# The low halves of 598 weight tiles: a negated copy on ScalarE and an accumulating DMA in place of a subtraction on VectorE

## The chip, the cores and the metric

The kernel runs on one core of a Trainium2 chip. The time is the device time of one execution in microseconds (us), lower is better. A core has a matmul engine (PE, with its weight loads shown apart as PEld), three engines for elementwise work (DVE is VectorE, ACT is ScalarE, POOL is GpSimd) and SP, which here only issues DMAs. POOL issues DMAs too; these go through the queue that the profile calls q0, software_dynamic, while SP's go through q1, hardware_dynamic. All queues share 16 DMA engines.

## The reference, cut to what matters

Two layers of a diffusion backbone on 512 latent and 256 context tokens with 1024 features, all float32. Each layer is a half-step SwiGLU FFN, a token mixer (a gated MLP in the first layer, attention in the second), and a second half-step FFN; every sublayer is modulated and closed by a layer norm.

```python
def swiglu(h, w_in, w_out):
    g, u = jnp.split(h @ w_in, 2, axis=-1)
    return (jax.nn.silu(g) * u) @ w_out

def ffn_sublayer(x, shift, scale, gate, w_in, w_out, ln_g, ln_b):
    y = swiglu(modulate(x, shift, scale), w_in, w_out)
    return layer_norm(ALPHA * x + 0.5 * gate * y, ln_g, ln_b)
...
        x_lat = ffn_sublayer(x_lat, ..., ffn_w_in[i, 0], ffn_w_out[i, 0], ...)
        x_ctx = ffn_sublayer(x_ctx, ..., ffn_w_in[i, 0], ffn_w_out[i, 0], ...)
        y_lat = gqa_mix(...) if is_attn else gmlp_mix(...)
        x_lat = layer_norm(ALPHA * x_lat + m_lat[5] * y_lat, ...)
        x_lat = ffn_sublayer(x_lat, ..., ffn_w_in[i, 1], ffn_w_out[i, 1], ...)
```

The output is the latent stream after both layers, so the last FFN runs on 512 tokens alone.

## The kernel before

A float32 operand is split in a high part, rounded to the type fp32r in which PE multiplies fast, and a low part, the rest. A product is three matmuls: high by high, high by low, low by high. Weights are split on the way. A unit is a 128x512 piece of a weight matrix, 256 KB: SP loads it into one of six `raw` buffers (`load_raw`), ScalarE copies it into the first half of one of eight `w` buffers (`split_later`, the copy of line 155), and VectorE subtracts that from `raw` into the second half (line 156). The subtraction is put in a list and written out at the next `flush`. The buffer `w` is free again when PE has multiplied with it, `raw` when both passes have read it. `units` yields the units in the order in which PE wants them, from a list of jobs that `__init__` makes: ("u", sources) is a plain run of pieces; "s" and "r" are Strassen steps of the FFN's first matrix, in which seven products take the place of eight and some units are sums made by VectorE (`sums`). Sources of `ffn_w_in` and of the first half of `gmlp_w_in` are cut as four runs of 128 floats for each of 128 partitions (runs of 512 bytes); sources of the output matrices, of `attn_w_qkv` and of gMLP's second half have rows of 2 KB.

PE's, SP's and POOL's instructions stay in the order in which the program writes them; a scheduler orders those of VectorE and ScalarE. POOL issues the DMAs of activations that are spilled and read back (`act<-stage`, `q<-act`), all-reduces and adds the pieces of the modulation vectors (`acc`, `mod`), raises variances to a power for the layer norms (`rs`), and issues the accumulating DMAs of the last residual (`zsum`, a buffer in DRAM, line 484).

The order of the work: a start of 100 us (modulation and the first units), layer 0's first FFN in Strassen steps to 370 us and its output matrix to 555, the gated MLP to 1157, layer 0's second FFN to 1730, layer 1's first to 2210, attention to 2440, and the last FFN, which has no Strassen steps ("latent FFN"), to 2817.

Of the kernel before, what the change touches and what calls it, by code (L numbers as in the profile page):

```python
# [8 lines left out]
F32R = mybir.dt.float32r  # L9
AF = mybir.ActivationFunctionType  # L10
ALU = mybir.AluOpType
AX = mybir.AxisListType

P = 128
D = 1024
KD = D // P
# [8 lines left out]
D_FF = 2816  # L25
# [14 lines left out]
W_BUFS = 8  # L40
# [53 lines left out]
class Backbone:  # L94
# [93 lines left out]
    def weight_order(self):  # L188

        io = self.io
        jobs = []

        def ffn(l, s, strassen=True, kernel_start=False):
            wi = io["ffn_w_in"][l, s].rearrange("(k p) f -> p k f", p=P)
            wo = io["ffn_w_out"][l, s]

            def cut(o, f, half):
                return wi[:, 4 * half : 4 * half + 4, o + f * P : o + f * P + P]  # L200

            start = FIRST_OPEN + SECOND_OPEN if kernel_start else OPEN
            if strassen:
                jobs.append(("u", [cut(0, f, half) for f, half in start]))
            for f in range(FF):
                if strassen:
                    srcs = [cut(0, f, 0), cut(D_FF, f, 0), cut(D_FF, f, 1), cut(0, f, 1)]
                    jobs.append(("r" if f < OPENED else "s", srcs))
                else:
                    jobs.append(("u", [cut(o, f, half) for o in (0, D_FF) for half in range(2)]))  # L210
            if strassen:
                through(wo, FF)
            else:
                order = Acts.orders(FF, KEPT_LAT, READ_BACK_LAT)[0]
                out(wo, order[:-CLOSE_LAT], 1)
                out(wo, order[-CLOSE_LAT:], CLOSE_LAT)

        def piece(wo, f, half):
            return wo[f * P : f * P + P, half * 512 : half * 512 + 512]

        def out(wo, order, n):
            for x in range(0, len(order), n):
                jobs.append(("u", [piece(wo, f, half) for half in range(2) for f in order[x : x + n]]))

        def through(wo, n):
            for half, order in enumerate(Acts.orders(n, KEPT, READ_BACK)):
                jobs.append(("u", [piece(wo, f, half) for f in order]))

        wm = io["w_mod"][0].rearrange("(k p) f -> p k f", p=P)
        quarter = lambda q: [  # L230
            wm[:, 2 * j : 2 * j + 2, i * D + q * 256 : i * D + q * 256 + 256] for i in (1, 0) for j in range(4)
        ]
        ffn(0, 0, True, True)
        first = jobs.pop(0)[1]
        start = quarter(0) + quarter(1) + quarter(2) + first[0:2] + quarter(3) + first[2:]
        jobs.insert(0, ("u", start))
        wi = io["gmlp_w_in"][0]
        for cc in range(GMLP_HALF // 512):
            o = GMLP_HALF + cc * 512
            jobs.append(("u", [wi[k * P : k * P + P, o : o + 512] for k in range(KD)]))  # L240
        wi = wi.rearrange("(k p) f -> p k f", p=P)
        us = lambda j: [wi[:, 4 * half : 4 * half + 4, j * P : j * P + P] for half in range(2)]
        for j in range(GMLP_CH):
            jobs.append(("u", us(j)))
        through(io["gmlp_w_out"][0], GMLP_CH)
        ffn(0, 1)
        ffn(1, 0)
        wq = io["attn_w_qkv"][0]
        for o in (1024, 0, 512):
            jobs.append(("u", [wq[k * P : k * P + P, o : o + 512] for k in range(KD)]))  # L250
        for h in (0, 4):
            out(io["attn_w_o"][0], range(h, h + 4), 4)
        ffn(1, 1, False)
        self.wsrc = [s for _, srcs in jobs for s in srcs]
        self.wraw, self.wready, self.wlive, self.raw_live, self.reserve = [], [], 0, 0, 0
        self.unit = self.units(jobs)

    def load_raw(self):
        while self.raw_live < RAW_BUFS and self.wsrc:
            src = self.wsrc.pop(0)  # L260
            raw = self.main.tile([P, 512], F32, tag="raw", bufs=RAW_BUFS, name="raw")
            dst = raw if len(src.shape) == 2 else raw[:, :].rearrange("p (a b) -> p a b", b=src.shape[2])
            self.sp.dma_start(dst, src)
            self.wraw.append(raw)
            self.raw_live += 1

    def take(self):
# [7 lines left out]
    def sums(self):  # L275
        return self.main.tile([P, 512], F32, tag="sums", bufs=2, name="sums")

    def unit_of(self, src):
        w = self.main.tile([P, 2, 512], F32R, tag="w", bufs=W_BUFS, name="w")
        self.split_later(w[:, 0], w[:, 1], src, w)  # L280
        if not self.slots:
            self.flush()
        return w

    def units(self, jobs):
        dve, w = self.dve, None
        for kind, srcs in jobs:
            if kind == "u":
                for _ in srcs:
                    w = self.unit_of(self.take())  # L290
                    self.drop(1)
                    yield w
                continue
            g1 = self.take()
            if kind == "s":
                yield self.unit_of(g1)
            u1, u2 = self.take(), self.take()
            if any(key is w for key, _ in self.lows):
                self.flush()
            s1, s2 = self.sums(), self.sums()  # L300
            dve.tensor_tensor(s1, u1, u2, ALU.add)
            dve.tensor_tensor(s2, s1, g1, ALU.subtract)  # L302
            yield self.unit_of(s2)
            dve.tensor_tensor(u1, g1, u1, ALU.subtract)
            w = self.unit_of(u1)
            self.drop(2)
            yield w
            yield self.unit_of(s1)
            g2 = self.take()
            if kind == "s":  # L310
                yield self.unit_of(g2)
            w = self.unit_of(u2)
            self.drop(1)
            yield w
            dve.tensor_tensor(s2, g2, s2, ALU.subtract)
            w = self.unit_of(s2)
            self.drop(1)
            yield w
# [207 lines left out]
    def need(self, *units):  # L526
        for u in units:
            while u not in self.mod_done:
                self.fill()
# [853 lines left out]
    def attention(self, l, i, nblocks, end, prev):  # L1383
# [172 lines left out]
        def step():  # L1556
            if queue and next(queue[0], self) is self:
                queue.pop(0)
                step()

        for n in range(len(units)):
            if n < 12 and n % 3 == 1:
                q_norm(1, n // 3)
            if n + AHEAD < len(units):
                sc = scores(n + AHEAD)
                todo = probs(n, state.pop(n))
                for f in todo:
                    f()
                state[n + AHEAD] = softmax(*sc)
            else:  # L1570
                for f in probs(n, state.pop(n)):
                    f()
# [486 lines left out]
```

## Time and profile before

| | us |
|---|---|
| median of 3 runs | 2817.7 (2817.39 to 2819.66) |
| span of the profiled execution | 2816.9 |
| PE busy | 2771.2 |
| VectorE busy | 2101.1 |
| ScalarE busy | 1163.0 |
| POOL busy | 537.4 |

The profiled execution has no other time beside its span, which lies 0.8 us below the median of the runs. A group's row names line, engine, operation and tiles (written, then read), the count, the busy time, the mean of one in ns, and the idle time of the engine ahead of it with what ended it. In a row of windows stand the stretch, its length, the busy time of each engine with its instructions, the granted PE clock, the DMA share and GB/s. A row of waits says who waited for whom: microseconds in all, times, longest. A row of the timeline starts with the start time and the length of a run of like instructions.

### The profile page before, as it was taken

The numbers are of one execution on the slowest core, as the hardware profiler recorded it, in microseconds if no ns is written. First come the engines' busy times: TensorE is split into PE (matmuls) and PEld (weight loads), VectorE is DVE, ScalarE is ACT, GpSimd is POOL, SyncE is SP. The second block draws the span as 40 slices with busy tenths as digits, with TensorE's granted clock in tenths as the row PEclk, the third lists the DMA queues.
The fourth block names the chain that finished last, engine by engine and source line by source line (L and its number), as shares of the span: only waits on it lengthen the run. The fifth ranks groups of instructions, "written<-read, shape, count | busy, mean of one in ns | idle before, by whom it ended". The sixth has DMA issues, their size and how long they took to land.

```text
span 2816.9 us, 40812 instructions
## 1 busy us (share of the span) xinstructions
PE 2771.2 (98%) x14478; PEld 2501.4 (89%) x14478; DVE 2101.1 (75%) x3681; ACT 1163.0 (41%) x2245; POOL 537.4 (19%) x605
## 2 busy tenths in 40 slices
PE   7999999999999999999999999999999999999998
PEld 5999988888899988899999889999988888888886
DVE  6988879587687776698888759888886598733445
ACT  6433432442355532463334236333432666623321
POOL 1001044333321232200102220000242121000001
PEclk9999999999999999999999999999999999999999
DMA  7443366366565474344336534434595524454352
GB/s 232 131 135 122 112 225 211 114 199 198 184 180 167 150 237 140 123 148 139 121 121 200 181 113 133 144 120 124 154 314 152 148 69 88 132 150 132 113 168 82
DMA packets 398819, 429.99 MB, mean 153 GB/s; under 512 B 28504, under 2 KB 288024, under 8 KB 398616
## 3 DMA queue, kind: packets, MB, share of 16 engines
q1 hardware_dynamic: 364504, 319.40, 37.0%
q0 software_dynamic: 34112, 108.00, 12.4%
q8 instruction: 113, 1.85, 0.3%
q14 instruction: 90, 0.74, 0.1%
HBM read 366.10 MB, written 63.41 MB: 152 GB/s over the span
## 4 chain that ended last, share of the span: by engine, by line
PE 86%; DVE 5%; issue 3%; ACT 3%; DMA 1%; POOL 1%; SPq 0%; DVEq 0%; POOLq 0%; ACTq 0%
PE ps L89 86%; DVE w L89 1%; DMA raw<-in_w_mod_dram 1%; PE pp L89 1%; POOL acc L383 0%; POOL rs L184 0%; ACT z L1957 0%; DMA raw<-in_ffn_w_in_dram 0%; DVE comb L89 0%; DVE w L156 0%; ACT h L601 0%; ACT p L1473 0%; ACT w L155 0%; ACT w L89 0%; DVE nm L1465 0%
## 5 line engine op out<-in xcount | busy, mean ns | idle before, releaser
L89 PE MATMUL ps<-comb,w 128*128 128x384 f32 x5544 | 972.2, 335 | 9.8 <-DVE q L89 2.6
L89 PEld LDWEIGHTS ps<-comb,w 128*128 128x128 f32 x5544 | 961.1, 188 | 16.8 <-DVE w L89 3.8
L89 PE MATMUL ps<-w,acts 128*128 128x512 f32 (+1 forms) x3792 | 860.1, 388 | 0.0
L89 PEld LDWEIGHTS ps<-w,acts 128*128 128x128 f32 x3792 | 707.3, 188 | 145.0
L89 ACT CAST w<-raw 128x512 fp32r<-128x512 f32 x630 | 387.7, 620 | 819.9 <-PE ps L89 723.2
L89 DVE TENSOR_TENSOR w<-raw,w 128x512 fp32r<-128x512 f32 x630 | 454.8, 729 | 260.0 <-ACT w L89 259.9
L89 PE MATMUL ps<-h,w 128*128 128x384 f32 (+2 forms) x2304 | 445.1, 353 | 0.2 <-DVE w L156 0.2
L89 PEld LDWEIGHTS ps<-h,w 128*128 128x128 f32 x2304 | 402.4, 188 | 37.8 <-DVE w L156 0.4
L89 DVE SCALAR_TENSOR_TENSOR acc<-mraw,cs,acc 128x512 f32<-128x512 f32 x378 | 279.2, 772 | 20.3 <-DMA mraw<-in_w_mod_dram 19.8
L89 PE MATMUL ps<-w,h 128*128 128x512 f32 x1200 | 274.6, 390 | 0.0
L383 POOL PARTITION_ALL_REDUCE acc<-acc x56 | 204.8, 3660 | 351.4 <-DVE acc L89 331.3
L89 PEld LDWEIGHTS ps<-w,h 128*128 128x128 f32 x1200 | 224.6, 188 | 46.3
L89 POOL DMA_DIRECT2D act<-stage x84 | 48.4, 576 | 973.5 <-DVE stage L89 934.6
L89 DVE TENSOR_TENSOR q<-q,ps 128x384 f32<-128x384 f32 (+1 forms) x258 | 143.7, 557 | 106.5 <-PE ps L89 89.3
L89 ACT CAST w<-sums 128x512 fp32r<-128x512 f32 x198 | 122.8, 620 | 237.8 <-DVE sums L302 118.1
L89 POOL DMA_DIRECT2D q<-act x226 | 129.0, 625 | 466.1 <-DVE acts L89 308.4
L89 ACT CAST acts<-q 128x384 fp32r<-128x384 f32 (+1 forms) x262 | 127.3, 519 | 78.9 <-DVE q L89 44.2
L89 DVE TENSOR_TENSOR acts<-q,acts 128x384 fp32r<-128x384 f32 (+1 forms) x262 | 145.5, 588 | 8.3 <-ACT acts L89 8.3
L89 DVE TENSOR_TENSOR w<-sums,w 128x512 fp32r<-128x512 f32 x198 | 140.2, 708 | 1.9 <-ACT w L89 1.9
L156 DVE TENSOR_TENSOR w<-raw,w 128x512 fp32r<-128x512 f32 x114 | 75.8, 688 | 28.8 <-ACT w L155 28.4
L184 POOL TENSOR_TENSOR rs<-ve,mhalf 128x1 f32<-128x1 f32 (+3 forms) x47 | 39.1, 831 | 274.8 <-DVE ve L181 167.7
L155 ACT CAST w<-raw 128x512 fp32r<-128x512 f32 x114 | 68.1, 627 | 48.3 <-PE ps L89 25.5
(203 smaller groups left out, 2162.4 us busy)
## 6 DMA issues: line engine op xcount, KB each, us to landing
raw<-in_ffn_w_in_dram SPq DMA_DIRECT2D x400, 256.0 KB, 3.0
mraw<-in_w_mod_dram SPq DMA_DIRECT2D x256, 256.0 KB, 3.5
raw<-in_ffn_w_out_dram SPq DMA_DIRECT2D x176, 256.0 KB, 3.4
q<-act POOLq DMA_DIRECT2D x216, 192.0 KB, 4.3
act<-stage POOLq DMA_DIRECT2D x74, 384.0 KB, 2.9
raw<-in_gmlp_w_in_dram SPq DMA_DIRECT2D x96, 256.0 KB, 3.3
zhat<-z POOLq DMA_DIRECT2D x26, 512.0 KB, 2.9
raw<-in_gmlp_w_out_dram SPq DMA_DIRECT2D x48, 256.0 KB, 2.9
```

Source lines behind the costliest of these rows:

```text
L89: return self.tc.keep_in_program_order(f(*args, **kwargs))
L155: self.act.copy(hi, src)
L156: self.lows.append((key, lambda: self.dve.tensor_tensor(lo, src, hi.bitcast(F32), ALU.subtract)))
L184: self.last_rstd = self.nc.gpsimd.tensor_tensor(rs, ve, self.mhalf[:, 0:1].to_broadcast([P, n]), ALU.pow).ins
L383: nc.gpsimd.partition_all_reduce(accs[c], accs[c], P, bass_isa.ReduceOp.add)
```

## The change

For 598 of the units the second half is made in another way. ScalarE writes the negated high half into it (a second pass, with a scale of −1, rounded as the first), and then POOL issues a DMA that reads the raw piece from DRAM once more and adds it there: raw − high. The units are all pieces of the plain jobs (kind "d" now) and the three unsummed ones of a Strassen step, g1, g2 and u2; the start's units, the Strassen sums and u1 stay with VectorE. 312 of the new DMAs have rows of 2 KB, 286 have four runs of 512 bytes for a partition.

```diff
-                    jobs.append(("u", [cut(o, f, half) for o in (0, D_FF) for half in range(2)]))
+                    jobs.append(("d", [cut(o, f, half) for o in (0, D_FF) for half in range(2)]))
...
         def out(wo, order, n):
             for x in range(0, len(order), n):
-                jobs.append(("u", [piece(wo, f, half) for half in range(2) for f in order[x : x + n]]))
+                jobs.append(("d", [piece(wo, f, half) for half in range(2) for f in order[x : x + n]]))
...
-            self.wraw.append(raw)
+            self.wraw.append((raw, src))
...
+    def unit_from(self, raw, src):
+        w = self.main.tile([P, 2, 512], F32R, tag="w", bufs=W_BUFS, name="w")
+        self.act.copy(w[:, 0], raw)
+        self.act.mul(w[:, 1], raw, -1.0)
+        low = w[:, 1] if len(src.shape) == 2 else w[:, 1].rearrange("p (a b) -> p a b", b=src.shape[2])
+        self.pool.dma_start(low, src, accum_op=ALU.add)
+        return w
...
-            if kind == "u":
+            if kind in ("u", "d"):
                 for _ in srcs:
-                    w = self.unit_of(self.take())
+                    raw, src = self.take()
+                    w = self.unit_of(raw) if kind == "u" else self.unit_from(raw, src)
...
-                yield self.unit_of(g1)
+                yield self.unit_from(g1, src)
...
-                yield self.unit_of(g2)
-            w = self.unit_of(u2)
+                yield self.unit_from(g2, src)
+            w = self.unit_from(u2, second)
```

POOL's order where layer 1 passes from the first FFN to attention, before: `rs` are the powers of the layer norm, `zsum` the last residual, which begins here with its bias.

```order
L184 TENSOR_TENSOR rs_21189<-ve_21188,mhalf 128x1
L184 TENSOR_TENSOR rs_21274<-ve_21273,mhalf 128x1
L89 DMA zsum_21297<-in_ln_b_dram 128x1024
L89 DMA zsum_21298<-in_ln_b_dram 128x1024
L89 DMA zsum_21299<-in_ln_b_dram 128x1024
L89 DMA zsum_21300<-in_ln_b_dram 128x1024
L484 DMA zsum_21297<-zraw 128x512
```

The same place in the changed kernel, where `w` is the second half of a unit:

```order
L184 TENSOR_TENSOR rs_21617<-ve_21616,mhalf 128x1
L89 DMA w<-in_attn_w_qkv_dram 128x512 x2
L184 TENSOR_TENSOR rs_21708<-ve_21707,mhalf 128x1
L89 DMA zsum_21731<-in_ln_b_dram 128x1024
L89 DMA w<-in_attn_w_qkv_dram 128x512 x4
L89 DMA zsum_21732<-in_ln_b_dram 128x1024
L89 DMA zsum_21733<-in_ln_b_dram 128x1024
L89 DMA zsum_21734<-in_ln_b_dram 128x1024
L495 DMA zsum_21731<-zraw 128x512
```

Six of the attention's first low halves now stand in POOL's order around the last power of the layer norm and the first bias.

ScalarE's order where attention ends and the latent FFN opens, before: line 155 is the copy of a unit, 1957 and 1947 normalise a token block (`z`), 601 modulates and 615 makes the tile `h` that PE multiplies.

```order
L1957 ACTIVATE z<-z,nb,rs_23701 128x1024
L615 CAST h<-q 128x4x128
L155 CAST w<-raw 128x512 x6
L601 ACTIVATE q<-ps,modB,modA 128x128 x8
L615 CAST h<-q 128x4x128 x2
L155 CAST w<-raw 128x512
L1947 ACTIVATE z<-z,nb,rs_23789 128x1024
L155 CAST w<-raw 128x512
```

And in the changed kernel (282 and 283 are the two passes of a unit, 1968 and 1958 the normalisations, 612 and 626 the modulation and `h`):

```order
L1968 ACTIVATE z<-z,nb,rs_24167 128x1024
L626 CAST h<-q 128x4x128
L282 CAST w<-raw 128x512
L283 ACTIVATE w<-raw 128x512
L282 CAST w<-raw 128x512
L283 ACTIVATE w<-raw 128x512
L282 CAST w<-raw 128x512
L283 ACTIVATE w<-raw 128x512
L282 CAST w<-raw 128x512
L283 ACTIVATE w<-raw 128x512
L612 ACTIVATE q<-ps,modB,modA 128x128
L1958 ACTIVATE z<-z,nb,rs_24259 128x1024
```

Where six copies stood ahead of the next token block's modulation there are four units of two passes, and the next normalisation now stands ahead of the rest of them.

More of the change, by code (lines that the diff above doesn't have):

```diff
@@ L222, in out @@
             for x in range(0, len(order), n):
-                jobs.append(("u", [piece(wo, f, half) for half in range(2) for f in order[x : x + n]]))
+                jobs.append(("d", [piece(wo, f, half) for half in range(2) for f in order[x : x + n]]))
         def through(wo, n):
             for half, order in enumerate(Acts.orders(n, KEPT, READ_BACK)):
-                jobs.append(("u", [piece(wo, f, half) for f in order]))
+                jobs.append(("d", [piece(wo, f, half) for f in order]))
         wm = io["w_mod"][0].rearrange("(k p) f -> p k f", p=P)
@@ L239, in weight_order @@
             o = GMLP_HALF + cc * 512
-            jobs.append(("u", [wi[k * P : k * P + P, o : o + 512] for k in range(KD)]))
+            jobs.append(("d", [wi[k * P : k * P + P, o : o + 512] for k in range(KD)]))
         wi = wi.rearrange("(k p) f -> p k f", p=P)
@@ L243, in weight_order @@
         for j in range(GMLP_CH):
-            jobs.append(("u", us(j)))
+            jobs.append(("d", us(j)))
         through(io["gmlp_w_out"][0], GMLP_CH)
@@ L249, in weight_order @@
         for o in (1024, 0, 512):
-            jobs.append(("u", [wq[k * P : k * P + P, o : o + 512] for k in range(KD)]))
+            jobs.append(("d", [wq[k * P : k * P + P, o : o + 512] for k in range(KD)]))
         for h in (0, 4):
@@ L293, in units @@
                 continue
-            g1 = self.take()
+            g1, src = self.take()
             if kind == "s":
-                yield self.unit_of(g1)
-            u1, u2 = self.take(), self.take()
+                yield self.unit_from(g1, src)
+            (u1, _), (u2, second) = self.take(), self.take()
             if any(key is w for key, _ in self.lows):
@@ L308, in units @@
             yield self.unit_of(s1)
-            g2 = self.take()
+            g2, src = self.take()
             if kind == "s":
-                yield self.unit_of(g2)
-            w = self.unit_of(u2)
+                yield self.unit_from(g2, src)
+            w = self.unit_from(u2, second)
             self.drop(1)
```

## The prediction

> **What bounds the kernel now.** I read the busy shares first, then the same numbers by stretch, then the chain of waits, the groups, the DMA issues, and last the timeline at the places where the matmul engine changes its work.
>
> ```profile
> span 2816.9 us, 40812 instructions
> PE 2771.2 (98%) x14478; PEld 2501.4 (89%) x14478; DVE 2101.1 (75%) x3681; ACT 1163.0 (41%) x2245; POOL 537.4 (19%) x605
> ...
> 100.00:2790.00 2690.00, 2676.94 (x13938) 2424.63 (x13938) 2010.78 (x3512) 1093.74 (x2108) 519.89 (x576) 1.00 0.49 152
> ...
> 2460.00:2560.00 100.00, 100.00 (x466) 83.80 (x465) 38.45 (x59) 29.24 (x49) 10.37 (x13) 1.00 0.52 153
> 2560.00:2690.00 130.00, 130.00 (x576) 107.63 (x575) 52.77 (x79) 42.80 (x71) 7.41 (x8) 1.00 0.39 118
> ...
> ACT w L89 <- PE ps L89: 803.2, 342, 14.3
> ...
> PEld ps L89 <- DVE w L156: 10.1, 22, 0.8
> ```
>
> PE is the bound: between 100 and 2790 us it is idle 2690 − 2676.9 = 13.1 us, at a granted clock of 1.00. So VectorE, though 75% busy, holds PE up almost nowhere: PE's weight load waits for low halves (the VectorE subtraction at line 156) 10.1 us in all, while ScalarE's copies wait 803.2 us for PE to free a weight buffer. Taking 598 subtractions off VectorE can therefore win at most those 13.1 us and a few at the start. What can be lost is larger: a low half that lands late stops PE, which has nothing else to do.
>
> **The change, part by part.** Of the weight units, 630 of them in the largest group below and the rest like them on other lines, 598 get their second half in the new way.
>
> ```profile
> L89 ACT CAST w<-raw 128x512 fp32r<-128x512 f32 x630 | 387.7, 620 | 819.9 <-PE ps L89 723.2
> L89 DVE TENSOR_TENSOR w<-raw,w 128x512 fp32r<-128x512 f32 x630 | 454.8, 729 | 260.0 <-ACT w L89 259.9
> ...
> L383 POOL PARTITION_ALL_REDUCE acc<-acc x56 | 204.8, 3660 | 351.4 <-DVE acc L89 331.3
> ...
> L484 POOL DMA_DIRECT2D zsum<-zraw x8 | 7.0, 872 | 66.2 <-DVE nm L1467 33.8 <-DVE zraw L477 14.4 <-DMA zsum<-q 7.2
> ...
> zsum<-in_ln_b_dram POOLq DMA_DIRECT2D x4, 512.0 KB, 10.3
> zsum<-zraw POOLq DMA_DIRECT2D x8, 256.0 KB, 4.8
> zsum<-q POOLq DMA_DIRECT2D x8, 256.0 KB, 4.1
> ...
> q0 software_dynamic: 144, 0.26, 46.1%
> ...
> q1 hardware_dynamic: 22267, 12.58, 42.1%
> ...
> raw<-in_ffn_w_in_dram SPq DMA_DIRECT2D x41, 256.0 KB, 3.3
> ```
>
> VectorE loses 598 × 0.729 = 436 us of work that mostly lay beside PE. ScalarE gains a pass of a 128x512 tile each; the copy of the same shape takes 0.62 us, so 598 × 0.62 = 371 us, and its busy time goes from 1163 to about 1534 of 2817 us: room enough, except where many units are made at once, 1.24 us instead of 0.62 apart. POOL issues 598 more DMAs; at the 0.87 us of the accumulating one, 521 us, so POOL comes to some 1060 us: room too, but its instructions stay in program order, so a low half can stand behind a 3.66 us all-reduce, and a pair of them costs 7.3.
>
> The accumulating DMA itself is shown only towards a buffer in DRAM (zsum, line 484); here the destination is on chip. Its landing takes 4.1 to 4.8 us there; a plain 256 KB load takes 3.3 in its busy row. I take 4.1, the smaller of the two rows, for the chip-side end, with 3.3 as the lower bound. Occupation of the engines: in a window of 4 us round one such DMA (2322.7 to 2326.7) the software queue held 46.1%, that is 1.84 us of all 16 engines. Plain loads in the 100 us window held 42.1 us for 41 weight and 8 modulation loads, 0.86 each. So a low half costs between 0.86 and 1.84 us of the DMA engines; 1.84 is nearest in kind, yet written to DRAM, and I take 1.7.
>
> The Trainium skill, "DMA: Bandwidth & Descriptors", section "Anatomy of one DMA — SWDGE (gpsimd) path", gives such a DMA 2.0 us plus its bytes at 436 GB/s, an estimate of 2.6 us here, and says that the wait for the write's receipt is longest when DRAM is the target. By that each of the four openings below would lose 1.5 us less, and the sum would be 34 instead of 40. The rows of this kernel say 4.1 to 4.8, so the row is taken.
>
> **In steady work** there are 8 weight buffers. The latent FFN takes 89 units in its 230 us (loads counted below), 2.6 us each, so a unit begun when its buffer comes free has 7 × 2.6 = 18 us until PE wants it. The new path takes 0.62 + 0.62 + issue 0.1 + 4.1 = 5.4 us, or 12.7 behind a pair of all-reduces: hidden. Other streams give more time for a unit. The cover is gone where PE begins on units just made, which happens at four places.
>
> ```profile
> 558.72 11.05 PE L89 MATMUL ps<-w,h 128*128 128x512 f32 x48
> ...
> 559.77 3.24 ACT L155 CAST w<-raw 128x512 fp32r<-128x512 f32 x6
> 560.45 3.71 DVE L156 TENSOR_TENSOR w<-raw,w 128x512 fp32r<-128x512 f32 x6 [0.84 <-ACT w L155]
> ...
> 2212.58 9.68 PE L89 MATMUL ps<-w,h 128*128 128x512 f32 x42
> ...
> 2213.64 3.25 ACT L155 CAST w<-raw 128x512 fp32r<-128x512 f32 x6
> ...
> 2439.80 3.25 ACT L155 CAST w<-raw 128x512 fp32r<-128x512 f32 x6
> ...
> 2442.01 8.65 PE L89 MATMUL ps<-h,w 128*128 128x256 f32 x70 [0.16 <-DVE w L156]
> ...
> 2448.45 1.25 ACT L1947 ACTIVATE z<-z,nb,rs 128x1024 f32<-128x1024 f32 x1 [1.05 <-DVE nb L735]
> ...
> 2773.83 16.48 PE L89 MATMUL ps<-w,acts 128*128 128x512 f32 x72
> ...
> 2776.75 4.02 ACT L89 CAST w<-raw 128x512 fp32r<-128x512 f32 x6 [14.29 <-PE ps L89]
> ```
>
> gMLP's opening: six units are cast in one run from 559.77. PE's matmuls take 11.05 / 48 = 0.230 us, six per unit here, two units were ready, so the first of the run is wanted at 558.72 + 12 × 0.23 = 561.5. Its low half lands at 559.77 + 1.24 + 4.1 = 565.1: 3.6 late. The later ones come 1.24 us (ScalarE) or 1.7 us (DMA) apart, PE takes 1.38 for each, so the sixth is 2.9 to 5.2 late. Term: 5.
>
> The attention opening is the same at 2213.64, 3.6 late, but on POOL a 512 KB bias copy for the residual (10.3 us to land) now stands between the second and third low half. Bounds 3.6 (it runs beside) and about 8; POOL's queue is one, so 7.
>
> The latent FFN's opening: at 2442.01 PE waits for a subtraction already. Its first low half lands at 2439.80 + 1.24 + 0.1 + 4.1 = 2445.2, 3.2 late. Units five to eight come on ScalarE behind a normalisation, eight activations and two copies; that normalisation runs at 2448.45 and moves with PE. So the stall grows to between 7 (if it does not move) and 11. Term: 10.
>
> The close: PE's 72 matmuls at 0.229 take eight units at 3 × 0.229 = 0.69 us each, 5.5 us; ScalarE makes them 1.24 apart (10 us), the DMAs 1.7 apart (13.6). PE ends 4.5 to 8 later. Term: 7.
>
> The three Strassen openings take their units singly, between long steps of PE; bounded by nothing and by one landing of 4.1 that nothing hides: 2.
>
> **DMA traffic** rises by 598 × 256 KB. In the latent FFN the shares above are 0.52 × 100 + 0.39 × 130 = 103 us of work in 230; its 74 + 15 weight loads (41 above, 33 and 15 in the second window) bring as many low halves.
>
> ```profile
> raw<-in_ffn_w_in_dram SPq DMA_DIRECT2D x33, 256.0 KB, 3.0
> raw<-in_ffn_w_out_dram SPq DMA_DIRECT2D x15, 256.0 KB, 2.6
> ```
>
> At 1.84 that is 103 + 164 = 267, 37 too many, less a lead of 18 − 5.4 = 13: 24 us lost. At 1.44 it fits. At my 1.7, 103 + 151 − 230 − 13 = 11. Term: 10 (0 to 24). The output projections and gMLP's first half are next:
>
> ```profile
> 375.00:530.00 155.00, 155.00 (x685) 128.07 (x684) 118.92 (x181) 47.55 (x94) 65.54 (x68) 1.00 0.64 207
> 560.00:760.00 200.00, 200.00 (x898) 166.33 (x897) 151.02 (x224) 65.63 (x115) 77.06 (x71) 1.00 0.60 195
> ```
>
> There PE takes 18 matmuls (six token blocks, three products) for a unit, at 155 / 685 = 0.226 us each 4.1 us: 38 units at 1.7 make 99 + 65 = 164 of 155, and 48 make 120 + 82 = 202 of 200; the lead of 7 × 4.1 − 5.4 = 23 us swallows that. Term: 3 (0 to 13).
>
> VectorE's relief: of PE's 13.1 idle us most are at the openings, which now wait for something else. Term −4 (−13 to 0).
>
> **Sum**: 5 + 7 + 10 + 7 + 2 + 10 + 3 − 4 = 40, so span 2816.9 + 40 = 2857, and 0.8 more as the median of the runs (2817.7) stands above this span: 2858.
>
> **Rivals.** *Short runs are dear* (0.17). 286 of the low halves are read in pieces of 512 bytes (all of ffn_w_in's). If the accumulation costs by the piece, one costs up to 4 × 1.84 = 7.4; the geometric middle of 1.84 and 7.4 is 3.7, and the latent FFN alone has 103 + 74 × 3.7 + 15 × 1.84 − 230 − 13 = 161 us too many: with the openings some 3005, and more from the Strassen stages. For it: plain 512-byte packets already cost 42.1 us × 16 / 22267 = 0.030 us each, a 2 KB accumulating one 1.84 × 16 / 144 = 0.20. Against: no row shows a price by the piece.
>
> The Trainium skill, "Collectives: The Full Stack", section "The bandwidth ceiling: the fold count and why AG ≠ RS ≠ AR", has accumulation half as fast since two sources are read, not for the addition. By that the piece would cost 2 × 0.86 = 1.7 and this rival falls; the 2 KB rows agree (1.84 against 0.86), no run here shows short ones.
>
> *Only the openings stall* (0.15): an on-chip destination costs 1.4 us or less, nothing is bound by DMA, and ScalarE's pace rules the openings: 4 + 5 + 8 + 5 + 1 − 4 = 19, 2837.
>
> *No change* (0.05): landings near 2 us and casts that come earlier, since ScalarE no longer waits for VectorE: 2818.
>
> *Faster* (0.05): VectorE's 436 us shorten its queue, so that the activations, h tiles and sums, which PE waits for, come earlier, and the 13.1 us vanish: 2804. It decides if a low half lands within 1.5 us of ScalarE's pass at the openings; the fastest comparable row is 4.1.
>
> **How the numbers follow.** The forecast, openings plus some DMA shortage (2838 to 2925), has 0.58. Within 0.2% (5.6 us, about what a measurement here can tell from no change) is 0.05, faster 0.05, slower 0.90. The range from 2830 to 2990 leaves out no change, faster, and half of the dear rival.
>
> **What would show it.** Right: idle PE before 561 to 568, 2215 to 2225, 2442 to 2455 and in the last 30 us, each ended by a DMA into w; VectorE near 1665 us busy; a DMA share close to 1 from 2460 to 2690 with PE below 100%. The dear rival shows in a software queue with over 3 us of all engines for each low half of ffn_w_in. I am wrong if PE's idle time stays at 13 us, or if it grows in the Strassen stages, for which I set only 2 us.

## The result: 5% slower, three and a half times the loss that was forecast

The changed kernel takes 2959.4 us (2955.6 to 2965.1, 4 runs) against 2818.7: a ratio of 1.0502, with a 95% interval of 1.0487 to 1.0517. The direction and the range were right. The forecast of 2858 was not: it has a loss of 40 us where there are 141.

The page of the changed kernel: its span, its busy times, the two queues and the issues of the DMAs, with the median time to landing in the last column.

```profile
span 2963.3 us, 42278 instructions
PE 2823.8 (95%) x14478; PEld 2529.9 (85%) x14478; DVE 1742.3 (59%) x3083; ACT 1474.1 (50%) x2843; POOL 1172.3 (40%) x1203
...
q0 software_dynamic: 230048, 264.80, 47.2%
q1 hardware_dynamic: 364504, 319.40, 35.8%
...
L89 POOL DMA_DIRECT2D w<-in_ffn_w_in_dram x238 | 310.4, 1388 | 528.7 <-ACT w L89 450.0
...
L89 POOL DMA_DIRECT2D w<-in_ffn_w_out_dram x176 | 169.8, 1017 | 231.1 <-ACT w L89 170.3
...
mraw<-in_w_mod_dram SPq DMA_DIRECT2D x256, 256.0 KB, 5.8
w<-in_ffn_w_in_dram POOLq DMA_DIRECT2D x238, 256.0 KB, 6.1
...
w<-in_ffn_w_out_dram POOLq DMA_DIRECT2D x176, 256.0 KB, 7.3
```

PE does the same 14478 matmuls, yet it is busy 2823.8 − 2771.2 = 52.6 us longer, and idle for 139.5 in place of 45.7, 93.8 longer. So over a third of the loss is no waiting at all: matmuls run slower. Windows of PE after a stall, with the granted clock third from the end of a row:

```profile
400.00:408.70 8.70, 8.70 (x40) 7.09 (x38) 0.00 (x0) 4.11 (x8) 1.42 (x2) 1.00 1.06 348
412.70:417.00 4.30, 4.22 (x10) 3.36 (x11) 4.05 (x8) 0.00 (x0) 3.38 (x6) 0.50 0.87 276
...
589.00:593.00 4.00, 3.52 (x8) 2.84 (x9) 0.78 (x2) 3.98 (x9) 0.41 (x2) 0.50 1.09 276
2194.00:2198.00 4.00, 3.62 (x9) 2.85 (x10) 4.00 (x8) 0.00 (x0) 0.00 (x0) 0.50 1.10 272
...
2260.00:2270.00 10.00, 10.00 (x45) 8.01 (x44) 3.40 (x11) 1.15 (x2) 0.84 (x1) 1.00 0.49 93
```

```profile
560.30:564.30 4.00, 4.00 (x16) 3.33 (x17) 0.16 (x1) 3.44 (x8) 1.57 (x3) 0.66 0.53 213
...
375.80:379.80 4.00, 4.00 (x23) 4.00 (x24) 1.26 (x3) 0.69 (x2) 0.84 (x1) 1.00 1.11 263
```

Each of the three rows at 0.50 begins where PE had stood still for 3.8 to 9.9 us, the row at 0.66 after 2.3 us, the one from 375.80 (still 1.00) after 1.6. In the 4 us after a long stall PE does 8 to 10 matmuls where the row from 2260 has 18, so in those 4 us alone such a stall costs some 2 us beyond its own length. The length does not decide it alone: a stall of 1.89 us in the Strassen steps, ended at 1280.27, was followed by the first row below, one of 2.44 us by the second.

```profile
1281.80:1285.20 3.40, 3.40 (x12) 3.40 (x11) 3.37 (x7) 1.14 (x2) 0.00 (x0) 0.50 0.91 152
...
2593.30:2597.30 4.00, 4.00 (x18) 3.29 (x19) 0.00 (x0) 1.15 (x2) 3.92 (x4) 1.00 1.31 214
```

The DMA share, last but one in a row, passes 1 in several rows here: packet times overlap, so a share of packet time is not the same as time for which the engines are taken.

PE's order is unchanged, so each matmul of one trace has its counterpart in the other, and the time between two of them can be compared by place. This table is worked out from the start times of the matmuls, in us; places by the times of the kernel before. It is of the profiled execution, the slowest of the four; its places add up to 148.8 where the span grew by 146.4 and the median by 141. In the runs below that leave the Strassen steps alone (4, 5, 6, 7, 9 and 10) the first row came out between 7.2 and 16.6, so a single value is good to some 5 us.

| place | forecast | changed kernel |
|---|---|---|
| first units and Strassen steps (to 370, 1229 to 1510, 1730 to 2035) | 2 | 14.7 |
| output matrices of the first and third FFN (370 to 555, 2035 to 2213) | under 3 | 19.1 + 28.0 |
| output matrices of gMLP and the second FFN (975 to 1157, 1510 to 1730) | 0 | 0.0 |
| gMLP, opening and first half (555 to 760) | 5 | 11.4 |
| gMLP, second half (760 to 975) | 0 | 8.8 |
| attention, opening (2213 to 2240) | 7 | 11.5 |
| attention, rest (2240 to 2440) | 0 | 14.6 |
| last FFN, opening (2440 to 2460) | 10 | 16.5 |
| last FFN, rest (2460 to 2690) | 10 | 8.9 |
| close (2760 to 2790) | 7 | 15.3 |

What PE waited for, from the chain of waits (microseconds in all, times, longest):

```profile
DVE acc L89 <- DMA mraw<-in_w_mod_dram: 126.1, 51, 12.1
...
PE ps L89 <- DMA w<-in_ffn_w_in_dram: 29.3, 17, 5.8
PE ps L89 <- DVE q L89: 13.6, 2, 9.9
PE ps L89 <- DMA w<-in_attn_w_qkv_dram: 10.2, 6, 5.6
PE ps L89 <- DVE acts L89: 10.2, 5, 3.8
PE ps L89 <- DMA w<-in_ffn_w_out_dram: 9.7, 8, 3.3
PE ps L89 <- DMA w<-in_gmlp_w_in_dram: 7.2, 4, 5.9
```

The rows on `w` are low halves that land late, as forecast. The rows on VectorE's `q` and `acts` are not: they lie in the output matrices. The timeline there (2180 to 2196) shows what VectorE does ahead of PE's longest stall:

```profile
2187.01 0.75 DVE L89 SCALAR_TENSOR_TENSOR acc<-mraw,cs,acc 128x512 f32<-128x512 f32 x1 [1.40 <-DMA mraw<-in_w_mod_dram]
2187.68 1.41 DVE L89 TENSOR_TENSOR z<-z,zraw 128x512 f32<-128x512 f32 x2
...
2192.97 0.75 DVE L89 SCALAR_TENSOR_TENSOR acc<-mraw,cs,acc 128x512 f32<-128x512 f32 x1 [3.88 <-DMA mraw<-in_w_mod_dram]
2193.64 2.48 DVE L89 SCALAR_TENSOR_TENSOR q<-ps,gate 128x512 f32<-128x512 f32 x4
...
2194.38 2.08 PE L89 MATMUL ps<-w,acts 128*128 128x512 f32 x4 [9.90 <-DVE q L89]
```

VectorE stands twice before a modulation load (`mraw`, for the next sublayer's vectors, which PE does not need yet). Behind it in VectorE's order stands `q<-ps,gate`, which empties PE's accumulation banks, and PE waits 9.90 us for one of them. Each VectorE instruction is short; its queue is late because loads are: 1.40 + 3.88 = 5.28 of the 9.90 us are these two waits.

### The profile page after: what moved, and what is told of

It reads as the page before. It is cut to its first block, busy times and chain, and to the rows that moved or that the text cites. A ratio compares the mean times of both kernels' runs of the same rounds, so it can differ in the third digit from the quotient of the medians.

```text
span 2963.3 us, 42278 instructions
## 1 busy us (share of the span) xinstructions
PE 2823.8 (95%) x14478; PEld 2529.9 (85%) x14478; DVE 1742.3 (59%) x3083; ACT 1474.1 (50%) x2843; POOL 1172.3 (40%) x1203
## 3 DMA queue, kind: packets, MB, share of 16 engines
q0 software_dynamic: 230048, 264.80, 47.2%
## 5 line engine op out<-in xcount | busy, mean ns | idle before, releaser
L89 PE MATMUL ps<-w,acts 128*128 128x512 f32 (+1 forms) x3792 | 879.9, 393 | 33.8 <-DVE q L89 13.6
L89 PEld LDWEIGHTS ps<-w,acts 128*128 128x128 f32 x3792 | 716.1, 191 | 189.8 <-DMA w<-in_ffn_w_out_dram 14.5
L89 ACT CAST w<-raw 128x512 fp32r<-128x512 f32 x630 | 389.1, 618 | 588.0 <-issue 410.0
L89 POOL DMA_DIRECT2D w<-in_ffn_w_in_dram x238 | 310.4, 1388 | 528.7 <-ACT w L89 450.0
L89 ACT ACTIVATE w<-raw 128x512 fp32r<-128x512 f32 x530 | 332.8, 628 | 0.0
L89 DVE TENSOR_TENSOR acts<-q,acts 128x384 fp32r<-128x384 f32 (+1 forms) x262 | 158.6, 631 | 251.9 <-ACT acts L89 246.3
L89 PE MATMUL ps<-w,h 128*128 128x512 f32 x1200 | 286.2, 399 | 17.5 <-DMA w<-in_attn_w_qkv_dram 10.2
L89 POOL DMA_DIRECT2D w<-in_ffn_w_out_dram x176 | 169.8, 1017 | 231.1 <-ACT w L89 170.3
L89 POOL DMA_DIRECT2D q<-act x226 | 154.3, 831 | 82.2 <-DVE acts L89 44.7
L89 POOL DMA_DIRECT2D w<-in_gmlp_w_in_dram x96 | 113.3, 1567 | 24.0 <-ACT w L89 9.2
```

Of the source, the lines that this page charges most:

```text
L89: return self.tc.keep_in_program_order(f(*args, **kwargs))
```

## The experiments

Times are medians. A difference with a plus sign is taken to the kernel before in the same call; what is called less or back is taken from the changed kernel's 2959.4.

**1 to 3: what of the new path costs.** The DMA is left out, made small, or made without the addition.

```diff
 e1  -        self.pool.dma_start(low, src, accum_op=ALU.add)
 e2  +        self.pool.dma_start(low[:, 0:64], src[:, 0:64], accum_op=ALU.add)   # as many columns of a cut piece
 e3  +        self.pool.dma_start(low, src)
```

> The second ScalarE pass stays, the DMA that adds the raw weight is left out (the low half holds only the negated high half). Theory T (the loss comes from the second read of the weights, through late low halves and through other loads made late): about 2818, between 2804 and 2825. Rival A (ScalarE's second pass holds things up): above 2860.

> The accumulating DMA is issued at the same places with the same waits, but adds 64 of a piece's 512 columns (32 KB in place of 256). Theory T: the stalls of the output projections (47 us) go, the openings keep half of theirs, since a small DMA still takes some 2 to 3 us to land: 2835 to 2855. Rival O (POOL's order: read-backs issued behind low halves that wait for ScalarE): nearly all of the loss stays, 2930 or more.

> The same DMA without the addition: it writes the raw weight over the negated half. Same bytes from DRAM, same waits. Theory T with a dear addition (1.7 to 1.84 us of the DMA engines against 0.86): about half of the loss stays, 2880 to 2900. If the bytes alone matter: 2940 to 2960. If the addition alone matters: below 2850.

Measured: without the DMA 2825.0 us (+7.0; 1.0026, 1.0016 to 1.0035; the upper end of the range expected), small 2849.6 (+31.6), plain 2875.9 (+57.9), the change itself +141. So the second ScalarE pass is no cause of weight (rival A falls), nor is POOL's order over the whole (rival O falls), though both are in the 32 us; for one place where POOL's order counts, see gMLP's second half below. Bytes and addition work together: cutting the bytes with the addition kept takes back 110, leaving out the addition with the bytes kept takes back 83, some 4 us more than was expected of a dear addition (2880 to 2900).

The software queue (packets, MB, share of the engines) in the kernel before, with the landing of the modulation loads there, then with the small DMA, then with the plain one:

```profile
q0 software_dynamic: 34112, 108.00, 12.4%
...
mraw<-in_w_mod_dram SPq DMA_DIRECT2D x256, 256.0 KB, 3.5
```

```profile
q0 software_dynamic: 120224, 127.64, 19.9%
```

```profile
q0 software_dynamic: 230048, 264.80, 36.3%
...
w<-in_ffn_w_in_dram POOLq DMA_DIRECT2D x238, 256.0 KB, 4.4
```

Before, this queue held 12.4% of 2816.9 us, 349. The change holds 47.2% of 2963.3, 1399, so one low half has (1399 − 349) / 598 = 1.76 us of packet time on all engines, if the queue's other DMAs cost what they did, plain (span 2873.6) 1.16, small (2847.0) 0.36. The same bytes with the addition have half as much again, and landed in 6.1 where the plain ones landed in 4.4. Each is taken under its own kernel's load, so how much of the half is the addition itself is not shown.

Where e1 loses its 7 us: 6.9 at attention's opening and 3.1 at the last FFN's, against 1.5 won at each of two Strassen openings, where VectorE is relieved. The waits of e1 name the first:

```profile
PE ps L89 <- DVE h L627: 4.1, 1, 4.1
```

Here the tile `h` is late, since on ScalarE its first half stands behind units that now take two passes.

**4 and 8: VectorE behind late modulation loads.** Four `mraw` buffers for three, in the changed kernel and in the one before.

```diff
-MRAW_BUFS = 3
+MRAW_BUFS = 4
```

> The changed kernel with four buffers in place of three for the modulation weights (mraw). Theory V (in the output projections VectorE stands before a late modulation load, and what PE waits for stands behind it in VectorE's order): of the 47 us lost there 15 to 30 come back, 2930 to 2945. Rival (PE waits there for activations read back, or for low halves): no change, 2955 to 2965.

> The kernel before, with four modulation buffers in place of three. Theory V: its VectorE waits for modulation loads too, but nothing that PE waits for is late: no change, 2815 to 2820. Rival (the fourth buffer helps by itself, so that the 28 us it brought to the changed kernel say nothing of the change): 2800 or less.

Measured: the changed kernel 2931.7, 27.8 less; the kernel before 2817.9 against 2817.9, nothing (0.9999, 0.9990 to 1.0009). By place, the two output matrices lose 9.6 and 17.0 in place of 19.1 and 28.0, gMLP's second half 0.5 in place of 8.8. VectorE's waits for modulation loads fall from 126.1 us to 64.2 in 28 waits. The other places move by under 2 us, but for the Strassen steps (9.0, within the spread named above). Of the 47.1 us in the two output matrices 26.6 are left, with 31.2 us of such waits there; a fifth buffer was not tried. In the first output matrix of the changed kernel, and then in the third FFN's, VectorE waits:

```profile
DVE acc L89 <- DMA mraw<-in_w_mod_dram: 20.3, 8, 12.1
```

```profile
DVE acc L89 <- DMA mraw<-in_w_mod_dram: 40.9, 18, 8.5
...
PEld ps L89 <- DVE q L89: 10.3, 1, 10.3
...
mraw<-in_w_mod_dram SPq DMA_DIRECT2D x39, 256.0 KB, 6.5
```

In the output matrices of gMLP and the second FFN, with 19 and 12 modulation loads in the stage for 28 and 39 here, the row is missing, and nothing is lost, though the DMA share (last but one) is as high there. The four stages in order of time, the first and the last of them losing:

```profile
373.00:577.00 204.00, 192.24 (x835) 157.52 (x835) 105.86 (x173) 84.91 (x164) 107.56 (x122) 0.97 0.84 233
1017.00:1199.00 182.00, 182.00 (x837) 153.83 (x836) 106.03 (x173) 83.08 (x161) 94.19 (x117) 1.00 0.91 251
1558.00:1778.00 220.00, 218.75 (x1033) 186.76 (x1032) 122.32 (x218) 112.50 (x221) 91.19 (x115) 1.00 0.78 219
2089.00:2295.00 206.00, 185.68 (x801) 150.91 (x801) 107.82 (x182) 82.79 (x161) 92.19 (x108) 0.96 0.83 239
```

But such a wait alone costs nothing; it counts where PE needs what stands behind it. The largest row, the first below, is gMLP's opening and first half (577 to 793), where PE's waits are for late low halves. The second is e1's, without the DMAs, in the third FFN's output matrix, which loses 0.0 there:

```profile
DVE acc L89 <- DMA mraw<-in_w_mod_dram: 61.1, 23, 6.3
```

```profile
DVE acc L89 <- DMA mraw<-in_w_mod_dram: 18.7, 10, 4.3
```

**5 and 9: the output matrices alone.** The 132 units of the three FFN output matrices go back to VectorE (e5), or keep the new path with a DMA of 64 columns (e9).

```diff
-                jobs.append(("d", [piece(wo, f, half) for f in order]))
+                jobs.append(("u" if n == FF else "d", [piece(wo, f, half) for f in order]))   # e9: "e", the small DMA
```

> Of the 598 units, the 132 of the three FFN output matrices in Strassen layers go back to VectorE's subtraction; the rest stays with the accumulating DMA. Theory V (traffic in those stages delays the modulation loads, VectorE waits for them in order, PE behind it): the 47 us lost in the first and third of them come back, and nothing elsewhere: 2905 to 2920. Rival (the loss there is carried over from the stages before, whose low halves are late): at most 15 us come back, 2945 or more.

> The changed kernel, with the accumulating DMA of the 132 units of the three FFN output matrices in Strassen layers cut to 64 of 512 columns: ScalarE's second pass, POOL's order and all waits stay, seven eighths of the added bytes go. Theory T (traffic delays the modulation loads there): as good as giving the units back to VectorE, 2918 to 2928. Rival O (POOL's order, ScalarE's pass): 2950 or more.

Measured: 2921.1 (1 us above the range) and 2924.4, that is 38.3 and 35.0 less than the change. The two places fall from 47.1 to 9.0 (e5) and 7.2 (e9). With ScalarE's pass, POOL's instruction and every wait still there, seven eighths of the bytes less do as much as taking the units back: it is the traffic.

**6 and 10: the openings and the close alone.** The 40 units on which PE begins at once go back to VectorE (e6), or get the small DMA (e10).

```diff
-                    jobs.append(("d", [cut(o, f, half) for o in (0, D_FF) for half in range(2)]))
+                    jobs.append(("u" if f < 2 else "d", [cut(o, f, half) for o in (0, D_FF) for half in range(2)]))
...
-                jobs.append(("d", [piece(wo, f, half) for half in range(2) for f in order[x : x + n]]))
+                jobs.append(("u" if n == CLOSE_LAT else "d", [piece(wo, f, half) for half in range(2) for f in order[x : x + n]]))
...                 # likewise the first 8 units of gMLP and of attention; e10: "e" for "u"
```

> 40 of the 598 units go back to VectorE's subtraction: the first 8 of gMLP, the first 8 of attention, the first 8 of the last FFN and the last 16 of the kernel. Theory (openings and close are lost to single low halves that land late, about 5 us each with the slow clock behind them): 40 to 50 us come back, 2905 to 2920. Rival (a saturated queue makes the next units late instead): under 20 us, 2940 or more.

> The same cut for the 40 units of the four openings and the close. If their loss is the landing time of full low halves under load, most of the 63 us comes back, 2900 to 2915; if a good part is ScalarE's second pass and the fixed time of any such DMA, about half, 2920 to 2935.

Measured: 2896.5 and 2927.9, that is 62.9 and 31.5 less. In e6, where 40 to 50 were expected back, the four places lose nothing: 40 of 598 units were 45% of the loss. In e10 they lose 5.1, 8.6, 7.1 and 4.3 in place of 11.4, 11.5, 16.5 and 15.3: half is landing under load, half is ScalarE's pace and what any such DMA takes. The expectation named both halves, and its second branch (2920 to 2935) holds.

**7: both sets.**

> Both sets of units, 172 of 598, go back to VectorE. If the two losses are separate, the gains add: 2855 to 2875, what is left being the Strassen stages (12), gMLP's first matrix (9) and attention (15). If they share a cause (the queue), less: 2885 or more.

Measured: 2858.5, 100.9 less; 38.3 + 62.9 = 101.2. The two losses are separate.

**11: two stages that lost nothing.** 92 units get the new path, gMLP's output matrix and the second FFN's; all others, the Strassen ones too, are subtracted by VectorE.

```diff
-                through(wo, FF)
+                through(wo, FF, "d" if (l, s) == (0, 1) else "u")
...
-        def through(wo, n):
+        def through(wo, n, kind="d"):
```

> The new low halves in two stages only, in which the changed kernel lost nothing: gMLP's output matrix (48 units) and the output matrix of layer 0's second FFN (44 units). Theory: a low half is hidden wherever eight buffers of lead and few modulation loads are there, so 2815 to 2821, no change. Rival (each such DMA costs a little, 141 us / 598 = 0.24): 2835 or more.

Measured: 2819.3 against 2818.7 (1.0002, 0.9993 to 1.0012): no change. In these two stages a low half made this way, with its lead and few modulation loads beside it, has no price of its own. No version here beats the kernel before.

## Why the prediction was wrong

**What holds.** PE is the bound, relief of VectorE is worth next to nothing (forecast −4; e1 wins 3.0 in the Strassen steps), two steady streams are hidden (e11), and PE stalls on low halves where gMLP, attention and the last FFN open and at the close. That 2959 lies in the range is luck in part: the range reached to 2990 for dear short runs, and these did not come. The DMA price taken was 1.7 us of the engines, where the runs have 1.76 of packet time, and the rest of the last FFN, forecast at 10 with that price, lost 8.9; no run takes that stretch apart, so the agreement may be luck as well. The rival of dear short runs is out: between 2600 and 2690, where 31 such low halves are issued,

```profile
q0 software_dynamic: 17272, 9.97, 77.1%
q1 hardware_dynamic: 17052, 9.89, 50.7%
```

77.1% of 90 us are 69.4, 2.2 each even if its other DMAs cost nothing, not 3.7. The two queues come to 127.8%, yet PE is busy 87.5 of these 90 us. The working treated a sum over 100% as time that PE must lose; packet times overlap, so that step is not borne out. The Trainium skill, "Collectives: The Full Stack", section "The bandwidth ceiling: the fold count and why AG ≠ RS ≠ AR", says of a reduction in a ring of cores that the addition halves the rate, by its second read; the runs have 1.76 against 1.16, a factor of 1.5, with both measured under load.

Three busy sums were off and decide nothing: VectorE lost 358.8 us and not 436, ScalarE gained 311.1 and not 371, since like instructions in a row overlap (the working's own row has six copies in 3.24 us), and POOL gained 634.9 and not 521. No row shows the 0.1 us for an issue.

**The term of 3 (0 to 13) for the output projections and gMLP's first half failed**, with 47.1 us in two output matrices alone. The working asked whether the DMA engines had room for the added bytes on average and found 164 of 155 us, swallowed by the lead of the weight buffers. That was right for the weights, which have seven units of lead, and it was asked of them alone. The modulation loads have three buffers and no such lead; their median landing goes from 3.5 to 5.8 us. In the kernel before VectorE waits for them too; its row from 372 to 555:

```profile
DVE acc L89 <- DMA mraw<-in_w_mod_dram: 7.6, 1, 7.6
```

That one wait did no harm; in the changed kernel there are 8 with 20.3 us in this stage and 18 with 40.9 in the third FFN's. The step that I left out is who stands behind such a wait: VectorE's queue, with the banks and activations that PE needs. e4 and e8 show it for 20.5 of the 47.1 us, and e9 that nearly all of them come from the added bytes.

**The openings' terms were too small**, 5 + 7 + 10 + 7 = 29 for 54.7. The mechanism was right at gMLP and at the close, where e1 loses nothing; at attention's opening e1, without any of the new DMAs, still loses 6.9 of the 11.5, where `h` stands behind units of two passes, and at the last FFN's 3.1 of 16.5. Two sizes were not right. First, the landing: I took 4.1 us from an accumulating DMA in a quiet stretch.

```profile
583.06 1.89 POOL L89 DMA_DIRECT2D w<-in_gmlp_w_in_dram  x2 [1.00 <-ACT w L283]
...
589.48 2.93 PE L89 MATMUL ps<-w,h 128*128 128x512 f32 x6 [5.85 <-DMA w<-in_gmlp_w_in_dram]
```

At gMLP's opening PE goes on 6.4 us after POOL issued the low half it waits for, 2.3 more than I took; my 3.6 us of lateness plus that makes 5.9, and 5.85 is there. The Trainium skill's 2.6 us estimate ("DMA: Bandwidth & Descriptors", "Anatomy of one DMA — SWDGE (gpsimd) path") is farther still: medians here are 6.1 to 8.9 under load. Second, the clock: from 589 to 595.7 it stands at 0.50 in the trace, 6.2 us of matmuls at half the pace, which adds some 3 us to the 5.85. I had counted each stall at its length. The Trainium skill has this rule ("TensorE: Matmul & The Clock Gate", "Part 1: The HAM clock gate (the "warmup" mystery)"): the clock falls to half after an idle window of about 3.4 us and comes back after as long a busy one, the window running on its own. The rows agree for the long stalls, 0.50 after 3.8 us and more. By that rule the stalls of 1.89 and 2.31 us, shorter than the window, would have left the clock alone, and they did not (0.50 and 0.66); the measurement decides. I had not priced the slow clock at all.

**Left out altogether**: gMLP's second half (8.8) and attention past its opening (14.6). e4 puts the first down to late modulation loads in part, since it leaves 0.5. But the wait that ends last there is POOL's order:

```profile
799.30 1.33 POOL L89 DMA_DIRECT2D w<-in_gmlp_w_in_dram  x1 [1.88 <-DMA w<-in_gmlp_w_in_dram]
808.82 1.37 POOL L184 TENSOR_TENSOR rs<-ve,mhalf 128x6 f32<-128x6 f32 x1 [8.19 <-issue]
...
812.84 0.58 PE L89 MATMUL ps<-w_sT,vn 128*128 128x256 f32 x1 [6.19 <-ACT vn L149]
```

PE waits for `vn`, which is made with the result of `rs`. The operand of `rs` was there at 795.76, but in POOL's order a low half stands ahead, issued at 799.30, and then POOL is idle for 8.19 us, for which the profile shows no cause. The kernel before has such an idle time too (7.20 us), but no low half ahead of it: there `rs` began 2.8 us after its operand, here 13.1. In e4 it is 6.0, and PE does not wait. So at this one place rival O has a part.

Attention's rest lost 0.7 with the small DMA and 6.5 with the plain one, so it needs the bytes too; which wait starts it was not taken apart. Of the Strassen steps' 14.7, against a forecast of 2, e2 leaves none and wins 3. That idle time grew in these steps is what the working named as a sign of being wrong; PE's wait there is for low halves:

```profile
L89 PE MATMUL ps<-comb,w 128*128 128x384 f32 x5544 | 978.0, 336 | 19.7 <-DMA w<-in_ffn_w_in_dram 14.3
```

**No change and faster** had 0.05 each, and neither came near: at the four places of the openings' terms the low halves took 6.1 us or more from issue to landing, where faster needed 1.5.

## What to carry to other kernels

When an edit adds traffic, do not only ask whether the engines have room and whether the new transfer is hidden: list every other load, with its own lead, and what stands behind its wait in the queue of the engine that waits. A load with three buffers can stop an engine that its own work would never stop. And a stall of the matmul engine is to be priced at its length plus the slow clock behind it, so a few units at the joins between stages can cost as much as all the rest.

## What the runs showed of the hardware

That the slow clock behind stalls of 1.9 to 9.9 us makes up 52.6 of the 146 us by which the span grew. And that the issuing engine pays for the addition: POOL took 1.02 us to issue an accumulating 256 KB DMA of 2 KB rows and 1.39 for one of 512-byte runs, against 0.60 and 0.77 for the plain ones (rows of e3 below, those of the change further up). With 64 of 512 columns added it still took 1.00 for the first kind, so it is not the bytes. That short runs cost POOL more is less sure: the attention's accumulating DMAs of 2 KB rows took 1.25 and 1.31.

```profile
L89 POOL DMA_DIRECT2D w<-in_ffn_w_in_dram x238 | 180.3, 766 | 606.4 <-ACT w L89 550.0
...
L89 POOL DMA_DIRECT2D w<-in_ffn_w_out_dram x176 | 102.7, 600 | 282.2 <-ACT w L89 235.8
```
